# The head of a decoder layer on one core: x in four loads, the c row spread by two K = 1 products, and another order on ScalarE and VectorE

## The chip, the core and the metric

The kernel runs on one core of a Trainium2 chip. The metric is the device time of one execution in microseconds (us). Before the change three executions took 319.98, 317.79 and 318.15 us, a median of 318.15. Engines are called as in the profile: PE is TensorE (matmuls), PEld its weight loads, DVE is VectorE, ACT is ScalarE, POOL is GpSimd, SP is SyncE; a "q" behind a name (SPq, ACTq) is the engine's own instruction queue, where loads are issued.

## What is computed

One layer of a hybrid attention block on 512 tokens of width 1024:

```python
mod = silu(c) @ w_ada + b_ada                  # c: (1, 1024), w_ada: (1024, 3072)
shift, scale, gate = split(mod, 3)
h = rms_norm(x, norm_gain) * (1 + scale) + shift
proj = h @ w_in                                # q, k, v, gates of two head groups
...                                            # sliding-window attention, sparse attention
out = x + gate * (concat(A, B) @ w_out)
```

All data are f32. Products that need the precision are made in three passes of rounded operands: high by high, high by low and low by high, where the low part is what rounding left.

## The kernel before

The program has a head, a middle and a tail. The head (lines 290 to 413) computes h for eight tiles of 128 channels, transposed (channel on the partition, 512 tokens in the row), and at once the first projection (q, k, v of group A, 768 columns, `first_proj`). The middle holds the other projections and the 44 attention slots, put between each other by a planner with costs in us, and ordered by the framework's scheduler. The tail (lines 1002 to 1018) is the last product and the residual.

All the code of the head stands under `in_order(tc)`: on each engine the instructions keep the order in which they are written. What matters of it here:

- **Loads.** SP issues them all: x in eight loads of 256 KB (L297), `first` (L298: the column of c, the biases, the gain and the identity), `bias` (L299), then for k = 0 to 3 the modulation weights of tile k in two loads of 512 KB (L205 for k = 0 and 1, L209 for the rest) and the projection weights `wst` of tile k in one of 384 KB (L213), and between the first two tiles the row of c, spread over 128 partitions by the load itself (`scrow`, L305, 512 KB written). A load whose buffer or semaphore is still in use holds SP, and so all loads behind it.
- **Sums of squares** (L325 to L330): ACT squares each tile of x, DVE adds four tiles at a time into `sacc`, and PE sums `sacc` over the partitions into `pr`. The last tile is done in halves. DVE then works out the reciprocal root in 8 small steps (`rsqrt`, L101 to L108), and PE turns it into a row for all partitions (`rbp`, L352).
- **Modulation.** Tiles 0 and 1 get theirs from PE: `mod_pe` (L230) multiplies by the column silu(c), ACT copies the result out as `macc` (L233), `mod_col` (L250) sums it over the partitions, and `mod_ab` (L255, L256) makes the two columns `AB`. Tiles 2 to 7 get theirs from DVE: `mod_rows` (L222) multiplies the weights, which lie in rows, by `scrow`, the row silu(c), and adds up, two instructions of 1024 elements for each tile. `scrow` is made at L373 (tanh on ACT) and L376 (DVE). The same row is used once more for `gate` in the middle (L690).
- **Tile k** (`new_tile`): ACT makes `hh` (h rounded) and `hf` (h) from the scaled x (`h_high`, L276); DVE does `mod_rows` of the next tile, `hl` = hf - hh (L279), scales the next tile of x (L270), and makes `swl`, the low part of the next weights (L265), whose high part `swh` is ACT's (L262).
- **First projection of tile k**: three passes n = 0, 1, 2 on PE (L286, L287), which need (hh, swh), (hh, swl) and (hl, swh). Behind pass 0 of tile 0 stands `mod_pe(1)`, behind pass 1 of tile 0 `mod_col(1)`.
- **Dummies** (L312): products of zeros on PE, counts in `ND`, written where PE would have nothing to do.
- **The bias line** (L343 to L348): one small product `pl`, two ACT copies and two stores to DRAM; the middle reads the line back from there.

## Time and profile before

| | us |
|---|---|
| median of three executions | 318.15 |
| the profiled execution, its own time | 317.5 |
| its span, first to last instruction | 315.7 |
| start of the first product of the head's projection (L286, tile 0) | 16.28 |
| start of the first `mod_rows` | 21.93 |
| first product of the middle's projections (L469) | 53.81 |

The profiled execution took 317.5 us, of which 315.7 are the span of its instructions; 1.8 lie around it. Times in the trace are us from the span's start. A row of the timeline is: start, duration, engine, line, operation, output <- input, shapes, count, and in brackets how long the engine stood idle before it and who released it. A row that merges several instructions (x2, x3) gives the time from the first's start to the last's end. The mean granted clock of PE over the span is 0.998.

### The profile page before, as it was taken

To read this page: it belongs to the slowest core of one execution; us is meant where nothing else is said; L and a number is where in the kernel's file an instruction comes from. 1 tells how busy PE (TensorE), PEld (TensorE's weight loads), DVE (VectorE), ACT (ScalarE), POOL (GpSimd) and SP (SyncE) were. 2 spreads that over 40 slices of the span, in tenths; PEclk is the share of its full clock that TensorE was granted. 3 is DMA by queue.
4 is the path that set the end of the run, shared out by engine and by line. 5 is a ranking of instruction groups with operands and counts; after the bars stand their busy time and mean duration, and the time that the engine had idled before them with its cause. 6 is when DMAs were issued, how large, how long until landed. Compare 5 with 4: busy or idle time off the path is not lost.

```text
span 315.7 us, 5779 instructions
## 1 busy us (share of the span) xinstructions
PE 306.7 (97%) x2097; PEld 250.9 (79%) x2098; DVE 237.2 (75%) x657; ACT 195.8 (62%) x472; POOL 3.9 (1%) x21
## 2 busy tenths in 40 slices
PE   8989999999999999999999999999999999999995
PEld 3568888788988999889873878788788878788883
DVE  3689999999966658898997998988686686544220
ACT  5576457668967674767917767788685867503000
POOL 0000000000000000000000000000000000000000
PEclk9999999999999999999999999999999999999999
DMA  7999967900390808170653004222420220243201
GB/s 242 375 412 411 408 233 223 322 2 0 100 335 22 282 2 275 32 260 2 197 187 118 1 2 133 69 66 70 134 69 0 69 66 3 81 151 111 90 33 66
DMA packets 28087, 44.63 MB, mean 141 GB/s; under 512 B 1771, under 2 KB 19340, under 8 KB 28060
## 3 DMA queue, kind: packets, MB, share of 16 engines
q1 hardware_dynamic: 26908, 42.18, 38.5%
q10 hardware_dynamic: 1152, 2.10, 2.1%
q8 instruction: 16, 0.26, 0.3%
q14 instruction: 11, 0.09, 0.1%
HBM read 42.13 MB, written 2.14 MB: 140 GB/s over the span
## 4 chain that ended last, share of the span: by engine, by line
PE 76%; DVE 10%; DMA 6%; ACT 4%; issue 2%; SPq 1%; POOL 0%; ACTq 0%; DVEq 0%; POOLq 0%
PE pj L469 29%; PE pj L459 9%; PE po L930 7%; PE s L855 7%; PE sq L286 7%; PE pt L913 4%; PE skv L287 3%; PE pt L903 3%; DMA wst_ring<-in_w_qkv_a 3%; PE s L588 3%; DVE qs L520 2%; DMA xTp<-in_xT 2%; DMA raw<-in_w_gate 2%; DVE kTb L538 1%; DVE wl L174 1%
## 5 line engine op out<-in xcount | busy, mean ns | idle before, releaser
L173 ACT ACTIVATE wh<-raw 128x512 fp32r<-128x512 f32 (+1 forms) x52 | 31.2, 636 | 13.5 <-PE pj L469 13.4
L174 DVE TENSOR_TENSOR wl<-raw,wh 128x512 fp32r<-128x512 f32 (+1 forms) x52 | 34.8, 689 | 5.2 <-ACT wh L173 3.4
L459 PE MATMUL pj<-wh,hh 128*128 128x256 f32 (+1 forms) x128 | 37.0, 289 | 0.0
L459 PE MATMUL pj<-wl,hh 128*128 128x256 f32 (+1 forms) x128 | 36.7, 287 | 0.1
L459 PE MATMUL pj<-wh,hl 128*128 128x256 f32 (+1 forms) x128 | 36.6, 286 | 0.0
L867 ACT ACTIVATE pp<-pp,nm 128x256 f32<-128x256 f32 (+2 forms) x48 | 29.3, 613 | 6.6 <-DVE nm L860 6.4
L469 PE MATMUL pj<-hh,wh 128*128 128x512 f32 x80 | 32.2, 402 | 0.0
L469 PE MATMUL pj<-hh,wl 128*128 128x512 f32 x80 | 32.0, 400 | 0.0
L469 PE MATMUL pj<-hl,wh 128*128 128x512 f32 x80 | 31.8, 398 | 0.0
L860 DVE CUSTOM_DVE_ANT_0 pp<-s,bias 128x256 f32<-128x256 f32 (+2 forms) x48 | 25.5, 551 | 3.6 <-PE s L855 3.5
L469 PE MATMUL pj<-yl,wh 128*128 128x512 f32 x64 | 25.3, 398 | 0.0
L469 PE MATMUL pj<-yh,wh 128*128 128x512 f32 x64 | 25.2, 396 | 0.0
L1017 DVE SCALAR_TENSOR_TENSOR fin<-pj,gate,xr 128x512 f32<-128x512 f32 x8 | 6.0, 751 | 25.5 <-PE pj L469 25.5
L469 PE MATMUL pj<-yh,wl 128*128 128x512 f32 x64 | 25.1, 394 | 0.0
L459 PEld LDWEIGHTS pj<-wl,hh 128*128 128x128 f32 x128 | 24.1, 188 | 0.4 <-DVE wl L174 0.3
L459 PEld LDWEIGHTS pj<-wh,hh 128*128 128x128 f32 x128 | 24.1, 188 | 0.3 <-issue 0.2
L459 PEld LDWEIGHTS pj<-wh,hl 128*128 128x128 f32 x128 | 24.1, 188 | 0.2 <-issue 0.2
L855 PE MATMUL s<-kTb,qs 128*128 128x256 f32 (+2 forms) x96 | 23.5, 356 | 0.0
L888 DVE TENSOR_SCALAR pp<-pp,rr,grev 128x256 f32<-128x256 f32 (+2 forms) x48 | 21.1, 476 | 0.7
L914 ACT COPY ptT<-pt 128x384 f32<-128x384 f32 (+1 forms) x32 | 15.7, 530 | 7.0 <-PE pt L913 6.7
L904 ACT COPY ptT<-pt 128x512 f32<-128x512 f32 (+1 forms) x28 | 15.5, 552 | 5.2 <-PE pt L903 4.9
L469 PEld LDWEIGHTS pj<-hh,wh 128*128 128x128 f32 x80 | 15.0, 188 | 3.8 <-issue 1.2
(232 smaller groups left out, 703.7 us busy)
## 6 DMA issues: line engine op xcount, KB each, us to landing
ada_ring<-in_w_ada_rows SPq DMA_DIRECT2D x12, 512.0 KB, 9.3
raw<-in_w_cmp SPq DMA_DIRECT2D x8, 512.0 KB, 6.5
raw<-in_w_gate SPq DMA_DIRECT2D x8, 512.0 KB, 5.6
raw<-in_w_o SPq DMA_DIRECT2D x8, 512.0 KB, 3.8
wst_ring<-in_w_qkv_a SPq DMA_DIRECT2D x8, 384.0 KB, 9.0
xTp<-in_xT SPq DMA_DIRECT2D x8, 256.0 KB, 4.9
ada_ring<-in_w_ada_cols SPq DMA_DIRECT2D x4, 512.0 KB, 7.3
bias<-line_d SPq DMA_DIRECT2D x8, 256.0 KB, 3.3
```

What stands on the lines that cost most here:

```text
L173: ACT.activation(wh, src, AF.Copy)
L174: DVE.tensor_tensor(wl, src, wh.bitcast(F32), op=OP.subtract)
L286: PE.matmul(pj_q[tb], lt, w[:, 0:512], start=f, stop=l, skip_group_check=True)
L459: PE.matmul(bank[:, t * n:(t + 1) * n], h[:, tb * 128:(tb + 1) * 128], w[:, k % 2, :], start=k == 0 and m == 0, stop=k == 7 and m == 2)
L469: PE.matmul(bank, w, h, start=k == 0 and m == 0, stop=k == 7 and m == 2)
L855: PE.matmul(ps, qs[h][:, 128 * i:128 * i + 128], k[:, hl_, lo:lo + w], start=hl_ == 0, stop=hl_ == 1)
L860: DVE.tensor_tensor_reduce(out=P[:, g, 0:w], in0=ps, in1=bt, scale=1.0, scalar=init, op0=OP.add, op1=OP.min, accum_out=nm[:, g:g + 1])
L867: ACT.activation(P[:, g, 0:e], P[:, g, 0:e], AF.Exp, bias=nm[:, g:g + 1], scale=-1.0, accum_out=dn[:, g:g + 1])
L888: DVE.tensor_scalar(v, v, rr[:, g:g + 1], gates[:, g, br:br + 1], op0=OP.mult, op1=OP.mult)
L904: ACT.copy(T[:, :, 0:nb, :], rev(pt[:, 0:2 * nb * 128].rearrange("p (g b q) -> p g b q", g=2, b=nb)))
L914: ACT.copy(T[:, 0:nb, :], rev(pt[:, 0:nb * 128].rearrange("p (b q) -> p b q", b=nb)))
L930: PE.matmul(o[64 * g:64 * g + 64, 128 * i:128 * i + 128], vb[:, 64 * g:64 * g + 64], sl["T"][g][:, b, :], start=first_of and b == 0, stop= ...
```

## The change

- x is laid out in DRAM as four blocks [128, 2, 512] and loaded in four loads of 512 KB, 4 KB for each partition, in place of eight with 2 KB. (The residual's loads of x in the tail read 2 KB out of each 4 KB.)
- `first` is padded from 168 to 256 columns.
- The row of c is loaded once, to one partition (4 KB), by ACT's own queue ahead of everything on ACT. ACT's tanh and DVE's product that make silu(c) run on this one partition ahead of the squares. PE multiplies a column of ones with K = 1 by the row, two products of 512 columns, into the banks `pj_q[0]` and `pj_q[1]`, and ACT copies them to `scrow` on all partitions behind `th`.
- `bias` is loaded behind the modulation weights of tile 0. Its product `pl` moves behind `mod_col(0)` into `pj_q[3]`, its copies and stores behind `hh(0)` and `hf(0)`.
- `weights_high(1)` (swh of tile 1) is written behind `mod_pe(1)`, so that ACT's copy `macc(1)` comes ahead of it; `weights_low(1)` (swl of tile 1) is written behind `mod_ab(1)`, so on DVE it comes behind `AB` of tile 1 and ahead of the first `mod_rows`.
- The dummies go from (20, 2, 2, 3, 4) to (10, 2, 2, 1, 2, 2); the sixth number is a group behind the K = 1 products.

```diff
-ND = (20, 2, 2, 3, 4)
+ND = (10, 2, 2, 1, 2, 2)
...
-        for k in range(8):
-            SP.dma_start(xT[k], A["xT"][k])
+        ACT.dma_start(scrow[0:1, :], A["c"])
+        for k in range(4):
+            SP.dma_start(xTp[:, 2 * k:2 * k + 2], A["xT"][k])
         SP.dma_start(first, A["first"])
-        SP.dma_start(bl, A["bias"])
         for k in range(NR):
             load_ada(k)
+            if k == 0:
+                SP.dma_start(bl, A["bias"])
             load_wst(k)
-            if k == 0:
-                src = A["c"]
-                SP.dma_start(scrow, bass.AP(tensor=src.tensor, offset=src.offset, ap=[[0, 128], [1, D]]))
...
         dummies(ND[0])
+        throw = T2(F32, "throw"), T2(F32, "throw")
+        for e in range(2):
+            v = scrow[0:1, 512 * e:512 * e + 512]
+            ACT.activation(throw[e][0:1, :], v, AF.Tanh, scale=0.5)
+            DVE.scalar_tensor_tensor(v, throw[e][0:1, :], 1.0, v, op0=OP.add, op1=OP.mult)
+        for e in range(2):
+            PE.matmul(pj_q[e], one_row, scrow[0:1, 512 * e:512 * e + 512], start=True, stop=True)
+        dummies(ND[5])
...
         ACT.activation(th, cT, AF.Tanh, scale=0.5)
+        for e in range(2):
+            ACT.activation(scrow[:, 512 * e:512 * e + 512], pj_q[e], AF.Copy)
...
-        PE.matmul(pl, bl[:, NEAR:NEAR + 40], bl[:, 0:NEAR], start=True, stop=True)
         dummies(ND[1])
-        ACT.copy(lsb[0:40, LINE - NEAR:LINE], pl)
...
         mod_col(0)
+        PE.matmul(pl, bl[:, NEAR:NEAR + 40], bl[:, 0:NEAR], start=True, stop=True)
         dummies(ND[3])
...
         h_low(0)
-        weights_high(1)
-        weights_low(1)
-        throw = T2(F32, "throw"), T2(F32, "throw")
-        for e in range(2):
-            ACT.activation(throw[e], scrow[:, 512 * e:512 * e + 512], AF.Tanh, scale=0.5)
-        for e in range(2):
-            v = scrow[:, 512 * e:512 * e + 512]
-            DVE.scalar_tensor_tensor(v, throw[e], 1.0, v, op0=OP.add, op1=OP.mult)
...
                 if k == 0 and n == 0:
                     mod_pe(1)
+                    weights_high(1)
                 if k < 7 and n == 1:
                     if k == 0:
                         mod_col(1)
                         mod_ab(1)
+                        weights_low(1)
                     new_tile(k + 1)
```

Three places show how the instructions now stand.

DVE, from hl of tile 0 to the first `mod_rows` (ISA rows; in the changed kernel lines are shifted by 2), before and then now:

```order
L279 TENSOR_TENSOR hl_84<-hf,hh_76 128x512
L265 TENSOR_TENSOR swl<-wst_ring,swh 128x768
L376 SCALAR_TENSOR_TENSOR scrow<-throw,scrow 128x512 x2
L255 TENSOR_TENSOR AB<-pj,first 128x1
L256 SCALAR_TENSOR_TENSOR AB<-pj,prm_98,first 128x1
L222 ISA ada_ring,AB<-ada_ring,scrow,first 128x1024
```

The same place on DVE in the changed kernel:

```order
L281 TENSOR_TENSOR hl_86<-hf,hh_78 128x512
L257 TENSOR_TENSOR AB<-pj,first 128x1
L258 SCALAR_TENSOR_TENSOR AB<-pj,prm_100,first 128x1
L267 TENSOR_TENSOR swl<-wst_ring,swh 128x768
L224 ISA ada_ring,AB<-ada_ring,scrow,first 128x1024
```

The two products of the row have left this place, and swl of tile 1 has moved from ahead of AB to behind it.

ACT, from h of tile 0 to h of tile 1, before and then now:

```order
L363 ACTIVATE hh_76<-xTp,AB 128x256 x2
L364 ACTIVATE rb<-pj 128x512
L365 ACTIVATE hf<-xTp,AB 128x512
L262 ACTIVATE swh<-wst_ring 128x768
L373 ACTIVATE throw<-scrow 128x512 x2
L233 ACTIVATE macc_309<-pj 128x256
L276 ACTIVATE hh_77<-xTp,AB 128x256 x2
```

The same place on ACT in the changed kernel:

```order
L370 ACTIVATE hh_78<-xTp,AB 128x256 x2
L371 COPY raw<-sq_124 40x256
L372 ACTIVATE rb<-pj 128x512
L373 ACTIVATE hf<-xTp,AB 128x512
L377 COPY raw<-raw 8x384
L235 ACTIVATE macc_295<-pj 128x256
L264 ACTIVATE swh<-wst_ring 128x768
L278 ACTIVATE hh_79<-xTp,AB 128x256 x2
```

The tanh of the row has left, macc of tile 1 is ahead of swh of tile 1, and the two copies of the bias line have come in between.

PE, from the first dummies to the sums of squares, now (before, twenty dummies stood there and nothing else):

```order
L313 MATMUL skv_125<-zero 128x512
L322 MATMUL sq_121<-scrow,one_row 128x512
L322 MATMUL sq_122<-scrow,one_row 128x512
L313 LDWEIGHTS zero
L313 MATMUL skv_125<-zero 128x512
L313 LDWEIGHTS zero
L313 MATMUL skv_125<-zero 128x512
L339 MATMUL pj<-ones,sq 128x1 x4
```

The two K = 1 products (operands `one_row` and one partition of `scrow`) stand on PE ahead of both sums of squares. In the middle, the scheduler orders the instructions of about 60 to 125 us a little differently: attention products and projection products change places with each other, with none added or left out; from about 130 us on the order is the same on all engines.

## The prediction

> **What bounds the kernel now.** I read the page first, then the stages, then the chain of waits, and only then single instructions. Two rows of stages: the head's inner tiles, and a piece of the middle (columns: stretch, its length, busy time of PE, PEld, DVE, ACT, POOL with counts, granted PE clock, DMA share, GB/s).

> ```profile
> 22.00:48.00 26.00, 25.96 (x144) 21.63 (x143) 26.00 (x42) 15.23 (x24) 0.00 (x0) 1.00 0.90 346
> 62.00:80.00 18.00, 17.01 (x126) 15.44 (x124) 17.39 (x40) 13.36 (x33) 0.68 (x4) 1.00 0.02 8
> ```

> From 22 to 48 us DVE is busy 26.00 of 26.00 us. PE's 25.96 look the same, but a busy PE counts the pipelined ends of its products; which of the two waits is read from single rows. Here are DVE from hl of tile 0 to the first `mod_rows`, the last `mod_rows` with its hl, and a place on PE:

> ```profile
> 17.94 0.69 DVE L279 TENSOR_TENSOR hl<-hf,hh 128x512 fp32r<-128x512 f32 x1
> 19.66 0.96 DVE L265 TENSOR_TENSOR swl<-wst_ring,swh 128x768 fp32r<-128x768 f32 x1 [1.03 <-ACT swh L262]
> 20.54 1.28 DVE L376 SCALAR_TENSOR_TENSOR scrow<-throw,scrow 128x512 f32<-128x512 f32 x2
> ...
> 21.93 1.28 DVE L222 CUSTOM_DVE_ANT_0 ada_ring<-ada_ring,scrow,first 128x1024 f32<-128x1024 f32 x1
> ...
> 44.66 1.27 DVE L222 CUSTOM_DVE_ANT_0 ada_ring<-ada_ring,scrow,first 128x1024 f32<-128x1024 f32 x1
> ...
> 47.13 0.68 DVE L279 TENSOR_TENSOR hl<-hf,hh 128x512 fp32r<-128x512 f32 x1
> ```
> ```profile
> 47.60 0.28 PE L287 MATMUL skv<-swl,hh 128*128 128x256 f32 x1
> 47.87 0.50 PE L286 MATMUL sq<-swh,hl 128*128 128x512 f32 x1
> ```

> Five tiles take DVE 44.66 - 21.93 = 22.73 us, 4.55 each, with no gap. PE starts a pair (L286, L287) every 0.35 us, 12 pairs in 4.2 us for a tile; at 47.60 it has its last pair of pass 1 and starts pass 2 at 47.87, when hl (47.13 + 0.68) is there. So in the tiles DVE leads, and the head ends when DVE's chain does: **what counts is the start of the first `mod_rows`, 21.93**. What held that back is in the chain of waits (start, length, what):

> ```profile
> 4.01 5.36 DMA xTp<-in_xT
> 9.39 0.33 SPq L205
> 9.76 8.99 DMA wst_ring<-in_w_qkv_a
> ...
> 19.53 1.13 ACT throw L373 x2
> 20.67 0.28 ACT macc L233
> 20.99 0.61 PE pj L250 x4
> ```

> The last x landed at 4.01 + 5.36 = 9.37. The weights of tile 1 landed at 18.75; swh, the tanh of the row and then macc(1) followed in ACT's order, so PE's `mod_col(1)` began at 20.99.

> **The change part by part.** *The end of x.* Rows of the stages of loading, and of what ACT, DVE and PE do with x:

> ```profile
> 1.50:3.50 2.00, 2.00 (x6) 0.76 (x5) 0.00 (x0) 0.65 (x2) 0.00 (x0) 1.00 0.86 262
> 3.50:5.00 1.50, 1.50 (x5) 0.45 (x3) 0.35 (x1) 1.12 (x2) 0.00 (x0) 1.00 0.76 247
> 10.50:19.00 8.50, 7.83 (x65) 4.73 (x67) 5.89 (x23) 4.60 (x9) 0.00 (x0) 1.00 1.03 416
> ```
> ```profile
> 8.70 1.49 DVE L327 TENSOR_TENSOR sacc<-sacc,sq 128x512 f32<-128x512 f32 x2 [1.01 <-ACT sq L325]
> 10.29 0.76 DVE L327 TENSOR_TENSOR sacc<-sacc,sq 128x256 f32<-128x256 f32 x2
> ```
> ```profile
> 7.43 0.63 ACT L325 ACTIVATE sacc<-xTp 128x512 f32<-128x512 f32 x1 [0.61 <-DMA xTp<-in_xT]
> ```
> ```profile
> 10.77 1.05 PE L330 MATMUL pj<-ones,sacc 128*128 128x1 f32 x8 [0.58 <-DVE sacc L327]
> ...
> 16.28 0.51 PE L286 MATMUL sq<-swh,hh 128*128 128x512 f32 x1 [0.34 <-ACT hh L363]
> ```

> x is 2.10 MB. Loads with 2 KB rows ran at 262 and 247 GB/s up to 5.0, loads with 4 and 3 KB rows later at 416. All of it at 416 from 1.8 on, plus 0.3 to land, would end at 7.2; no better than now at 9.4. I take the first two rates up to 5.0 (0.52 + 0.37 = 0.89 MB), then 416 for the other 1.21 MB (2.9 us), and 0.2 to land: 8.1, nearer the fast end because the slow stretch is the start-up. But the last load now brings two tiles: after it come a square (0.63), its sum (half of 1.49, 0.74) and the first half's sum (0.38), 1.75 us to the start of PE's sum, where 10.77 - 9.37 = 1.40 stood. So PE's sum starts at 9.9, 0.9 earlier (9.0 to 11.15 for the two bounds). The steps from there to the first product at 16.28 are a chain of small ones and stay as they are.

> *The row of c.* The tanh's 1.13 us leave ACT's place ahead of macc(1), and its products' 1.28 leave DVE's ahead of `AB`. They come back ahead of the squares, on one partition, DVE's part ahead of its first sum; I cost them the same, since the length of a row and not the partitions set it in this pair of rows (8 partitions, 384 columns, against 40 and 256):

> ```profile
> 12.41 0.36 ACT L345 COPY raw<-sq 40x256 f32<-40x256 f32 x1 [2.19 <-PE sq L343]
> 12.81 0.51 ACT L346 COPY raw<-raw 8x384 f32<-8x384 f32 x1
> 13.98 0.38 ACT L233 ACTIVATE macc<-pj 128x256 f32<-128x256 f32 x1 [0.66 <-PE pj L230]
> ```

> The cover is the wait for x: if c lands at 2.9, the tanh ends at 4.0, where the first pair of x lands now anyway, and six squares end at 7.8, just ahead of x's last pair. So x at 7.2 would be used from 7.8 only, which caps this gain at 1.2; c later than 3.2 costs its lateness one for one. No row shows so small a load; those of 256 KB that ACT issues near the end take 2.9 us (line of the DMA issues: KB each, median us to landing):

> ```profile
> xr<-in_xT ACTq DMA_DIRECT2D x8, 256.0 KB, 2.9
> ```

> Issued at 0.8 that is 3.7 at the worst side (0.5 lost); at the best 1.8, before which no byte of x moves either (nothing more won). I take 2.9. [...]

> The copies of the row from PSUM, two of 512 columns at no more than a square's 0.63, lie in ACT's 2.19 + 0.66 us of idleness ahead of macc(0), so nothing; without that cover they would cost 1.3 us.

> *The loads behind x.* All come 1.3 us earlier by x, and those behind the old 512 KB of `scrow` another 1.3 (at 416 GB/s); the padding of `first` gives 0.1 back. The weights of tile 1 then land near 16.3, and ACT does not wait for them. SP's stores of the bias line wait for an ACT copy that ends at about 17.9, ahead of the 19.4 at which SP came there before, so the later loads on SP's queue aren't held.

> *Up to the first `mod_rows`.* ACT's last step of tile 0 and PE's `mod_pe(1)` ahead of pass 1 stand in these rows:

> ```profile
> 17.10 0.80 ACT L365 ACTIVATE hf<-xTp,AB 128x512 f32<-128x512 f32 x1
> ```
> ```profile
> 17.87 1.07 PE L230 MATMUL pj<-ada_ring,scz 128*32 128x256 f32 x16
> ```

> Pass 0 of tile 0 starts at 16.28 - 0.9 = 15.4. The bias copies put rb, hf and hl(0) 0.36 later (the copy with 40 partitions) and what follows hf 0.51 more: hl(0), 17.94 + 0.69 before, is done at 18.1, and ACT is free for macc(1) at 17.9 - 0.9 + 0.36 + 0.51 = 17.9. `mod_pe(1)` ends at 18.94 - 0.9 = 18.05, so macc(1) is there at 18.45, ahead of pass 1's end. So `mod_col(1)` starts as soon as pass 1, four pairs or 1.4 us, is through: 18.94 + 1.4 = 20.35 in the old order, now 19.5. From the start of `mod_col` to behind AB it was 21.93 - 20.99 = 0.94, so AB is done at 20.45. There the edit takes part of its gain back: **swl of tile 1, 0.88 from start to next start, now stands between AB and `mod_rows`**, while DVE idles from 18.1 to 20.2. The first `mod_rows` starts at 21.35 in place of 21.93: **0.6 earlier**, 0.3 less than PE's sum. PE's third pass gains more (19.95 against 21.46), but meets DVE's chain again in tile 1.

> *Dummies and K = 1 products.* Twelve dummies less; a product costs PE only where something waits behind it, which is a rival below.

> *The middle* gets the same work in another order. I take 0. PE's idle time there is 0.99 us in the row of 62 to 80 at the top, and that of these two:

> ```profile
> 125.00:150.00 25.00, 24.06 (x209) 22.70 (x208) 22.70 (x59) 18.03 (x41) 0.19 (x1) 1.00 0.32 112
> 150.00:175.00 25.00, 24.38 (x145) 16.81 (x144) 21.28 (x62) 15.82 (x41) 0.00 (x0) 1.00 0.46 159
> ```

> 2.55 us together (25 less 24.06 and 24.38); an order gains no more of what these rows show, and I let a bad one lose 1.3, half of that.

> **Sum.** 0.6 less (bounds -0.7, if x ends as now, to 0.9, for c's cap). The profiled execution took 317.5, so 316.9; the median of the runs, 318.15, gives 317.5. I say **317.5**.

> **The rivals.** *(a) The sums of PE come late: slower.* The K = 1 products stand ahead of both sums on PE, and PE's clock starts slow:

> ```profile
> 6.75 0.15 PEld L312 LDWEIGHTS <-zero 128*128 128x128 bf16 x1 [0.28 <-issue]
> 7.07 0.96 PEld L312 LDWEIGHTS <-zero 128*128 128x128 bf16 x5 [0.17 <-issue]
> 11.75 0.62 PE L343 MATMUL sq<-raw 33*40 33x256 f32 x2
> ```

> Dummies come every 0.43 us (0.15 and 0.28 of idleness of the weight load) up to 7.07, and five in 0.96 us from there. The f32 product of 256 columns takes two parts, 0.21 apart, so one of 512 takes 0.86 fast, 1.7 slow. Ten dummies end at 5.5. If the clock rises at 7.07 as before, the products end near 8, in time for 9.9. If it stays slow, they end at 8.9, two dummies at 9.8, the first sum (0.95 before) at 11.7, two dummies at 12.5: 2.6 late, all of it on the path. The rise decides this: from about 8 us on PE is the later one. With the 0.6 of the forecast lost and more: 318.15 - 0.6 + 2.6 = 320.2. Against it: PE is no emptier up to 5.5 than before. [...]

> *(b) x lands no earlier.* The same bytes on the same 16 engines; for it speaks the slow stretch up to 5.0, against it that 0.76 and 0.86 of DMA share there are idleness and not load. The first `mod_rows` then comes 0.7 later than before: 318.9.

> *(c) The new order of the middle closes most of its gaps*: 2 of 2.55 us: 315.5. For it: 62 to 80 has DVE nearly full and PE idle for 1 us. Against: an order that a scheduler makes has no reason to.

> **How the numbers follow.** Chances: the forecast 0.62, (a) 0.12, (b) 0.13, (c) 0.13. The forecast with the bounds of the head (-0.7 to 0.9) and half of the middle's is 316.0 to 319.0; to leave out no more than 2 in 10, the range goes half-way into (a) and (c): **315.6 to 319.6**. A measurement of this kernel can tell about 1%, 3.2 us, from no change. Faster by more needs (c) and the best head: 0.07. Slower by more needs (a) with a bad order: 0.05. Within 1%: 0.88.

> **What would show it.** Right: ACT's last square ends near 9.5; L286 of tile 0 starts near 15.4; PE doesn't wait ahead of `mod_col(1)`; DVE idles about 2 us ahead of AB of tile 1 and then has swl; the first `mod_rows` starts near 21.35; tiles 4.55 us apart; the first L469 near 53.2. Wrong: a first `mod_rows` ahead of 20.9 or behind 22.5, tiles closer than 4.5 us, or a middle from 53 to 271 us that changes by over 1.3.

## The result, and the profile after

| | executions | median us | lowest to highest | ratio to before, 95% interval |
|---|---|---|---|---|
| before | 15 | 318.05 | 317.02 to 319.98 | |
| after | 15 | 321.66 | 319.04 to 323.98 | 1.0081 [1.0053, 1.0108] |

The change costs 0.8%, about 2.6 us by the ratio and 3.6 between the medians, where 0.6 less was forecast. The profiled execution of after took 322.68 us, with a span of 320.9 (before 317.5 and 315.7). Ratios leave out executions more than 1.5% above the fastest of their kernel; that goes for one execution of after and of e1 and for two each of e2, e8 and e9, and the profile of e9 is of such a one (325.1 us).

The page's row of the granted clock, 40 slices of 8 us, in tenths of full speed:

```profile
PEclk9569999999999999999999999999999999999998
```

Slices two and three (8 to 24 us) show 5 and 6: half speed for most of them. The granted clock rises at 4.99 us, falls at 8.40 and rises again at 22.05. The first step is 3.41 us and the second four times that; a step of 3.41 us is called a window here. The stages around it (the columns are those of the prediction's stages; the number ahead of the last two is the granted clock):

```profile
5.00:8.40 3.40, 3.40 (x14) 1.43 (x12) 2.08 (x3) 1.69 (x4) 0.00 (x0) 1.00 0.92 323
8.40:22.00 13.60, 12.17 (x52) 7.58 (x52) 7.26 (x25) 7.30 (x16) 0.00 (x0) 0.50 1.02 391
...
24.00:28.00 4.00, 4.00 (x25) 3.52 (x24) 2.60 (x6) 2.96 (x6) 0.00 (x0) 1.00 0.37 119
28.00:50.00 22.00, 21.82 (x117) 17.62 (x116) 22.00 (x34) 12.25 (x20) 0.00 (x0) 1.00 0.99 355
```

The profiled execution is one of four with a share (the mean granted clock over the span) of 0.976, 322.2 to 322.7 us. Two have 0.982 (321.5 and 321.7 us), five 0.986 to 0.989 (319.0 to 320.2 us), and four have 0.998 or 1.00 and still took 321.5 to 324.0 us.

For 13.6 us the granted clock is 0.50, in the very stretch in which every step of the head waits for a short product of PE. From 28 us on DVE is full again (22.00 of 22.00), as before. PE itself (start, length, what, number of products; L313 are the dummies, called fillers from here on):

```profile
1.35 4.11 PE L313 MATMUL skv<-zero 128*128 128x512 bf16 x10 [1.35 <-DVE wst_ring L296]
5.39 1.98 PE L322 MATMUL sq<-scrow,one_row 1*128 1x512 f32 x4
7.30 0.61 PE L313 MATMUL skv<-zero 128*128 128x512 bf16 x2
7.75 1.30 PE L339 MATMUL pj<-ones,sq 128*128 128x1 f32 x8
8.91 1.01 PE L313 MATMUL skv<-zero 128*128 128x512 bf16 x2
11.35 1.86 PE L339 MATMUL pj<-ones,sacc 128*128 128x1 f32 x8 [1.43 <-DVE sacc L336]
```

PE was busy without a break through the window that ended at 8.40, but what it did in the middle of it were the two products with one row (L322, "1x512"). Behind it the same sum that took 1.05 us before (L330, x8) takes 1.86. The chain of waits up to `mod_pe(1)`:

```profile
1.65 6.43 DMA xTp<-in_xT
...
11.35 1.86 PE pj L339 x8
13.22 0.88 PE skv L313 x2
14.09 1.87 PE pj L232 x16
15.96 1.05 PE pj L358 x4
17.01 0.85 PE skv L313 x2
17.86 0.65 PE pj L252 x4
18.50 1.00 PE sq L361 x2
...
22.41 1.00 PE pj L232 x16
```

Before, this piece of the chain held x, the weights of tile 1, ACT's rounding, tanh and macc. Now it is PE alone, one slow product behind the other, the fillers too. The x on it is the third load, landed at 8.08; the fourth landed at 9.34, when DVE was still adding up the third (9.28 on), so the two come to nearly the same. DVE behind that:

```profile
21.52 0.69 DVE L281 TENSOR_TENSOR hl<-hf,hh 128x512 fp32r<-128x512 f32 x1
25.40 0.16 DVE L257 TENSOR_TENSOR AB<-pj,first 128x1 f32<-128x1 f32 x1 [3.18 <-PE pj L252]
25.47 0.21 DVE L258 SCALAR_TENSOR_TENSOR AB<-pj,prm,first 128x1 f32<-128x1 f32 x1
25.60 0.95 DVE L267 TENSOR_TENSOR swl<-wst_ring,swh 128x768 fp32r<-128x768 f32 x1
26.46 1.28 DVE L224 CUSTOM_DVE_ANT_0 ada_ring<-ada_ring,scrow,first 128x1024 f32<-128x1024 f32 x1
...
49.20 1.27 DVE L224 CUSTOM_DVE_ANT_0 ada_ring<-ada_ring,scrow,first 128x1024 f32<-128x1024 f32 x1
```

DVE idles 3.18 us ahead of A and B of tile 1, then does swl, then `mod_rows`, in the order that was foretold, but at 26.46 and not at 21.35. The span cut at starts of instructions, all from the traces (`e3` and `e5` are experiments, told below; before, the first product of the middle starts at 53.65 by its own row, and 53.81 is where the chain has it):

| stretch, us | before | after | e3 | e5 |
|---|---|---|---|---|
| start to PE's second sum of squares | 10.77 | 11.35 | 11.15 | 11.29 |
| to pass 0 of tile 0 | 5.51 | 8.25 | 5.40 | 5.50 |
| to `mod_col(1)` | 4.71 | 5.26 | 4.12 | 4.83 |
| to the first `mod_rows` | 0.94 | 1.60 | 1.60 | 0.94 |
| to the first product of the middle | 31.72 | 31.80 | 31.77 | 31.72 |
| to the end | 262.06 | 262.63 | 262.86 | 261.77 |
| span | 315.71 | 320.89 | 316.90 | 316.05 |

Of the 5.2 us between the two profiled spans 4.5 lie ahead of the first `mod_rows`, and 2.7 of these in the one stretch from PE's second sum to pass 0.

### The profile page after: what moved, and what is told of

Same layout as the page of the kernel before. It is cut to its first block, busy times and chain, and to the rows that moved or that the text cites. A ratio compares the mean times of both kernels' runs of the same rounds, so it can differ in the third digit from the quotient of the medians.

```text
span 320.9 us, 5766 instructions
## 1 busy us (share of the span) xinstructions
PE 310.8 (97%) x2090; PEld 253.1 (79%) x2090; DVE 237.4 (74%) x658; ACT 196.5 (61%) x474; POOL 3.9 (1%) x21
## 4 chain that ended last, share of the span: by engine, by line
PE 63%; DVE 22%; DMA 6%; issue 4%; ACT 3%; SPq 0%; DVEq 0%; ACTq 0%
PE pj L474 24%; PE po L935 7%; PE pj L464 7%; PE s L860 7%; PE pt L918 4%; DVE wl L176 4%; PE pt L908 3%; PE s L593 2%; DMA wst_ring<-in_w_qkv_a 2%; DVE ada_ring L224 2%; DVE qs L525 2%; DMA xTp<-in_xT 2%; DMA raw<-in_w_gate 2%; PE po L941 1%; DVE pa L865 1%
## 5 line engine op out<-in xcount | busy, mean ns | idle before, releaser
L1022 DVE SCALAR_TENSOR_TENSOR fin<-pj,gate,xr 128x512 f32<-128x512 f32 x8 | 6.0, 751 | 25.4 <-PE pj L474 25.4
L909 ACT COPY ptT<-pt 128x512 f32<-128x512 f32 (+1 forms) x28 | 15.4, 552 | 7.1 <-PE pt L908 6.0
## 6 DMA issues: line engine op xcount, KB each, us to landing
bias<-line_d SPq DMA_DIRECT2D x8, 256.0 KB, 4.1
```

The costliest lines, as they stand in the source:

```text
L909: ACT.copy(T[:, :, 0:nb, :], rev(pt[:, 0:2 * nb * 128].rearrange("p (g b q) -> p g b q", g=2, b=nb)))
```

## The experiments

Each kernel was timed beside the kernel before on the same chip; its ratio is to that. Three theories were named ahead of the first kernels. **A**: the products with one row don't keep the clock up; behind a window of 3.41 us with them in it, it falls, though PE is busy. **B**: only the share of PE's busy time decides, and the rows don't matter. **C**: the clock is not the cause; loads or order are.

**e1_fill**: the changed kernel with ten fillers, not two, between the sums of squares.

```
-ND = (10, 2, 2, 1, 2, 2)
+ND = (10, 2, 2, 1, 10, 2)
```

> The changed kernel with 8 more dummies (10 in place of 2) behind the first sum of squares; the K = 1 products stay. Theory A (products with K = 1 do not keep PE's clock up: the 3.4 us in which they stand count as idle, and the clock falls there, whatever stands behind): the clock still falls near 8.4 us in most executions, 320 to 322 us. Theory B (what counts is how much of the time PE works on anything; the idle 1.9 us ahead of the second sum and the missing dummies let it fall): the clock holds, the first mod_rows starts at 22.3 to 23, 318.2 to 319.3 us. Theory C (the clock is not the cause, but the loads and the order are): as the changed kernel, 321 to 322 us, even where the clock holds.

Measured: 321.69 us (320.09 to 326.0), ratio 1.0072 [1.003, 1.0114]: no better. PE's stages (columns: PE busy, granted clock, DMA share, GB/s) and its first rows:

```profile
5.00:8.40 3.40, 3.40 (x5) 1.00 0.91 333
8.40:16.80 8.40, 8.40 (x27) 1.00 1.03 378
```
```profile
1.35 4.45 PE L313 MATMUL skv<-zero 128*128 128x512 bf16 x10 [1.35 <-DVE wst_ring L296]
5.73 3.77 PE L322 MATMUL sq<-scrow,one_row 1*128 1x512 f32 x4
```

Here the clock column must not be believed: the trace records changes of the clock, the first in this execution is its rise at 16.86 us, and what lies ahead of the first is shown as 1.00. The durations tell the truth: four parts of the row products take 3.77 us (1.98 in after, at full speed), so the clock was low from the start. PE was busy for 8.40 of 8.40 us from 8.40 on and stayed slow. Theory B falls.

**e2_k128**: the changed kernel, with 128 rows in the two row products: the same row of c, which DVE's product now writes to `crow`, and 127 rows of zeros.

```
-one_row = con.tile([1, 128], F32, name="one_row")
+one_row = con.tile([128, 128], F32, name="one_row")
+crow = con.tile([128, D], F32, name="crow")          # zeroed ahead
-    PE.matmul(pj_q[e], one_row, scrow[0:1, ...], ...)
+    PE.matmul(pj_q[e], one_row, crow[:, ...], ...)
```

> The changed kernel with the two products of the row made with K = 128: the row in partition 0 of a tile whose other 127 rows are zeros, the same columns and the same place. Theory A: the 3.4 us with the products now count as work; the clock falls one such window later at the earliest, or where PE idles ahead of the second sum: 319 to 320.5 us, with 0 to 3 slow windows where the changed kernel has 2 to 4. Theory B: K does not matter, as the changed kernel, 321 to 322 us. Theory C: 321 to 322 us.

**e3_k128_fill**: both edits, 128 rows and ten fillers.

> Both edits together: products with K = 128 and 10 dummies behind the first sum. Theory A and theory B: the clock holds from its rise on, the first mod_rows starts at 22.3 to 23 us, 318.2 to 319.3 us in all. Theory C: 321 to 322 us with the clock up.

Measured: e2 319.78 us (317.38 to 322.81), ratio 1.0015 [0.9976, 1.0054]; e3 318.80 (318.2 to 319.65), ratio 0.9994 [0.9971, 1.0017], with a granted clock of 0.998 or more in all ten executions. PE's stages, e2 first:

```profile
6.00:12.90 6.90, 5.10 (x34) 1.00 1.02 356
12.90:16.30 3.40, 3.18 (x23) 0.50 1.03 408
```
```profile
6.00:12.90 6.90, 6.67 (x42) 1.00 1.02 355
12.90:16.30 3.40, 2.91 (x28) 1.00 1.03 413
```

With 128 rows but little filler, PE is busy for 5.10 of 6.90 us and loses the clock for one window at 12.90; with both, 6.67 of 6.90, it keeps it. e3 does the whole of the change's work in the change's order, and its first `mod_rows` starts at 22.27 and not at 26.46:

```profile
22.27 1.28 DVE L225 CUSTOM_DVE_ANT_0 ada_ring<-ada_ring,scrow,first 128x1024 f32<-128x1024 f32 x1
```

So C falls, and what is left is A; e9 and e12 below test it alone. In the profiled executions **the clock is 4.2 of the head's 4.5 us.** As the ratios go, 1.0081 against 0.9994, it is 0.9% of the time.

**e4_x4**: the kernel before, with x in four loads and nothing else.

> The kernel before with one part of the change: x in four loads of 4 KB rows (and the residual's loads of it in the tail with 2 KB rows at a pitch of 4 KB). If four loads bring x no earlier (as the changed kernel's trace has it: 9.3 us): the second sum starts 0.4 to 0.6 us later, since two tiles now hang on the last load, 318.2 to 318.7 us. If the larger rows are faster by themselves, and the changed kernel lost that to something else (the load of c on ACT's queue, or an earlier start of the modulation weights): x lands by 8.5 us, and the kernel is 0 to 0.5 us faster than before.

Measured: 318.53 us (317.16 to 320.6), ratio 0.9986 [0.9955, 1.0016]: nothing that can be told from none. ACT's squares:

```profile
7.95 0.61 ACT L325 ACTIVATE sq<-xTp 128x512 f32<-128x512 f32 x1
8.86 1.24 ACT L325 ACTIVATE sq<-xTp 128x512 f32<-128x512 f32 x3 [0.30 <-DMA xTp<-in_xT]
```

The last pair of x is there at 8.86 and PE's second sum starts at 10.80, against 10.77 before: what the last load won, two tiles in it took back. Whether it won anything isn't shown: with eight loads the last x lands between 8.85 (e12) and 9.87 us (e5).

**e5_before_fill**: the kernel before, with six more fillers between the sums.

```
-ND = (20, 2, 2, 3, 4)
+ND = (20, 2, 2, 3, 10)
```

> The kernel before with six more filler products between the two sums of squares (ND[4] 4 to 10) and nothing else. Theory A (the granted clock of the head is what separates executions, and the changed kernel lost it through the products with one row): the filler closes PE's idle stretch between the sums, so the clock stays up in all executions; the mix of clock shares that the kernel before shows (0.998, 0.994, 0.989) becomes 0.998 throughout, the first mod_rows stays within 0.3 us of 21.93, and the median falls from 318.4 to about 317.2, ratio 0.996. Rival (the slower executions of the kernel before come from something else than idle PE ahead of 12 us): the mix of clock shares and the median stay, ratio 1.00. Six more instructions in the head also move the written-out order of the middle; if that order is worth something by itself, the time between the first middle product and the end differs from 262.06 us by up to 1.3 us either way.

Measured: **317.20 us** (316.66 to 318.68, 12 executions), ratio 0.9958 [0.9937, 0.998]. The 35 executions of the kernel before that were timed beside it show clock shares of 0.989 (10), 0.994 or 0.995 (21) and 0.998 or more (4); a window of 3.41 us at half speed takes 0.54% off the share, so by this estimate these are two, one and none. All 12 of e5 show 0.997 or more. Theory A foretold this: the kernel before lost, by the same estimate, a window or two in most of its executions as well, and with six more products of zeros none of the 12 did. The first `mod_rows` lay at 22.56, since x was later by 0.5 in this execution, and the stretches behind are those of before.

**e6_swl**: e3 with `weights_low(1)` back ahead of A and B of tile 1.

```
                     mod_pe(1)
                     weights_high(1)
+                    weights_low(1)
...
                         mod_ab(1)
-                        weights_low(1)
```

> The changed kernel with 128 rows in the spread and the filler (the one that held its clock), and the low half of the second tile's weights put back ahead of that tile's A and B. Theory: what is left of its head behind the kernel before (22.27 against 21.93 at the first mod_rows) is the 0.95 us of that subtraction between A and B and mod_rows; ahead of A and B it runs from the end of the rounding at 20.56, in time in which VectorE waits, so the first mod_rows comes at 21.65, 0.6 us earlier, and the first middle product with it (53.4 against 54.04); the rest to the end stays or moves by up to 1 us with the middle's order: span 315.5 to 317. Rival: the gain is lost because A and B then wait for the subtraction as long as mod_rows did before (first mod_rows within 0.2 of 22.27), span 316.9.

Measured: 318.73 us (318.27 to 319.22), ratio 1.0017 [0.9995, 1.0038]. From PE's second sum to the first `mod_rows` it is 10.49 us in place of 11.12 in e3: the 0.6 are there, as expected. They are not in the time: from the first product of the middle to the end it is 263.20 in place of 262.86, though only this one instruction was moved.

**e7_order**: e5 with tile 1's rounding behind `mod_pe(1)`, so that macc need not wait for it.

```
-        weights_high(1)
-        weights_low(1)
...
                     mod_pe(1)
+                    weights_high(1)
+                    weights_low(1)
```

> The kernel before with the filler and one part of the change alone: the second tile's weights are rounded behind its modulation sums, so that macc no longer waits for the rounding; c, x and the bias stay as before. Theory: macc runs at about 19.2 in place of 20.57, the second tile's mod_col comes when pass 1 ends (about 20.4), VectorE's subtraction (about 21.3) is then what A and B wait for, first mod_rows at 21.5 (21.93 before), so the order alone is worth 0.4 us of the head. Rival: silu(c)'s spread row, which still takes its two Tanh on ScalarE and two products on VectorE in the same stretch, leaves the first mod_rows where it was, 21.9; then the order and the spread's removal are only worth something together.

Measured: 317.22 us (316.9 to 317.97), ratio 0.9965 [0.9945, 0.9984]. The first `mod_rows` starts at 21.17, 10.34 us behind PE's second sum (e5: 11.27). The median is that of e5: what the head wins here (0.93) is not in the time, and from the first product of the middle to the end e7 takes 262.29 where e5 takes 261.77.

**e10_bias** is e7 with the change's place for the bias row, its two copies behind `hh` and hl of tile 0; **e11_spread** is e7 with c's row spread as in e2 (128 rows), with ten fillers at the start and two behind the products in place of twenty.

> The kernel before with the filler and the weights' order, and the change's place for the bias row added: its load behind the first modulation weights, its product behind the first mod_col, its two copies and two stores behind. Theory M1 (the 0.8 us that all kernels with the whole change take longer from the first middle product to the end, 262.5 to 263.2 against 261.8 to 262.3, come from the bias row's later copies and stores): 262.8 here, time 317.8 to 318.2. Theory M2 (they come from the written-out order of the middle, which any edit of the head shifts): somewhere between 261.7 and 263.2, not bound to this edit; time 317.2 with the head at 52.9.

> The kernel before with the filler and the weights' order, and the spread added: c as one row by the other queue, two products with 128 rows, the spread load, the two wide Tanh and two wide products gone. Theory: ScalarE and VectorE lose 1.13 and 1.28 us of work ahead of the second tile's A and B, so macc and the rounding can run by 0.3 us earlier, but the second tile's mod_col stays behind pass 1 on PE (20.3), and the first mod_rows comes at 21.2 as without the spread: worth nothing, 317.2. Rival: the 512 KB less in the queue ahead of the second tile's weights and the free VectorE bring it to 20.8 or less, 316.8. If the middle's 0.8 us come with the spread (M3), 262.8 from the first middle product to the end and 318.0.

Measured: e10 318.03 us (317.56 to 318.56), ratio 0.9998 [0.9987, 1.001]; e11 317.71 (317.15 to 318.55), ratio 0.9983 [0.9966, 1.0001]. ACT of e7, then of e10:

```profile
17.05 0.80 ACT L365 ACTIVATE hf<-xTp,AB 128x512 f32<-128x512 f32 x1
17.76 1.14 ACT L371 ACTIVATE throw<-scrow 128x512 f32<-128x512 f32 x2
18.95 0.39 ACT L233 ACTIVATE macc<-pj 128x256 f32<-128x256 f32 x1
19.23 0.84 ACT L262 ACTIVATE swh<-wst_ring 128x768 fp32r<-128x768 f32 x1
```
```profile
16.65 0.35 ACT L361 COPY raw<-sq 40x256 f32<-40x256 f32 x1
...
18.23 0.51 ACT L367 COPY raw<-raw 8x384 f32<-8x384 f32 x1
18.76 1.15 ACT L372 ACTIVATE throw<-scrow 128x512 f32<-128x512 f32 x2
19.82 0.37 ACT L233 ACTIVATE macc<-pj 128x256 f32<-128x256 f32 x1
20.09 0.83 ACT L262 ACTIVATE swh<-wst_ring 128x768 fp32r<-128x768 f32 x1
```

The two copies of the bias row used to lie in ACT's idle stretch behind the squares. In the new place they stand ahead of the tanh, macc and the rounding swh. macc is not what counts: `mod_col(1)` starts 9.36 us behind PE's second sum, and 9.49 in e7. swh starts 9.01 behind it in place of 8.40, and swl, A and B and `mod_rows` follow it on DVE: the first `mod_rows` moves from 10.34 to 10.94. That is 0.6 lost, of the 1.05 us between the two ratios, whose intervals don't meet; the rest isn't placed. The spread wins nothing here: 10.37 in e11. M1's time (317.8 to 318.2) came true, but by luck: its cause falls, for the middle does not take longer (262.31 us from the first middle product to the end in e10, 262.29 in e7, 262.45 in e11).

**e8_k32_fill**: e3 with 32 rows in the row products, the same order on every engine.

> As the kernel with 128 rows in the spread and the filler, with the same order of instructions on every engine but 32 rows in the two row products (one with data, 31 of zeros). Theory A1 (what the throttle counts grows with the rows that a product uses, so a quarter of the rows is too little): the clock falls in the window that holds them as it did with one row, half clock for one to four windows of 3.41 us ahead of 20 us, time 319.5 to 322. Theory A2 (one row alone is special; a row group of 32 already counts as busy): the clock holds as with 128 rows, clock share 0.998 in all runs and 318.8 median.

Measured: 318.87 us (318.45 to 325.33), ratio 1.003 [1.0006, 1.0054]. Neither quite: of the eight executions in its ratio six are as e3's (318.45 to 318.91), and two lost one window (320.08 and 320.59, share 0.995). The other two of its ten took 325.2 and 325.3, which no kernel with 128 rows came to. In e3 and e6, with 128 rows, none of twenty lost one.

**e9_k1_alone** and **e12_k128_alone**: the kernel before with the fillers of e5, and with two row products of zeros, whose result is thrown away, in place of the last ten fillers of the start. They differ in the rows of that product alone, and PE's order is the same.

```
 dummies(ND[0])                       # 10 in place of 20
+for e in range(2):
+    PE.matmul(pj_q[2 + e], one_row, zrow, start=True, stop=True)   # 1 row in e9, 128 in e12
```

> The kernel before with ten more fillers taken as follows: of the twenty at the start the last ten give way to two row products of one row each (zeros, result thrown away, waiting for nothing), and the filler between the two sums has its six more. No other part of the change is in it. Theory A: two products with one row in place of ten fillers take the granted clock away again, half clock in at least one window of 3.41 us between 7 and 20 us in most executions, median 318.3 to 321.5. Rival (the clock was lost by the wait for c, by PE's later sums or by the order, none of which is in here): clock share 0.998 or more throughout and 317.2, as with the fillers.

> The same kernel with 128 rows of zeros in the two products, the same order of instructions on every engine. Theory A: the clock holds in all executions, 317.2 median (317.0 to 317.6). Rival: no difference from the one with one row.

Measured: e9 318.81 us (318.38 to 325.13), ratio 1.0025 [1.0003, 1.0046]; e12 **317.13** (316.7 to 318.95), ratio 0.9963 [0.9933, 0.9992]. PE in e9, then in e12:

```profile
1.90 4.45 PE L316 MATMUL skv<-zero 128*128 128x512 bf16 x10 [1.90 <-DVE wst_ring L298]
6.27 3.78 PE L320 MATMUL sq<-zrow,one_row 1*128 1x512 f32 x4
9.98 1.87 PE L336 MATMUL pj<-ones,sq 128*128 128x1 f32 x8
```
```profile
1.91 4.45 PE L316 MATMUL skv<-zero 128*128 128x512 bf16 x10 [1.91 <-DVE wst_ring L298]
6.15 2.42 PE L320 MATMUL sq<-zrow,one_row 128*128 128x512 f32 x4
8.41 0.95 PE L336 MATMUL pj<-ones,sq 128*128 128x1 f32 x8
```

Both start slow (4.45 us for ten fillers; the next ten of e12, behind the rise, take 2.32). In e12 the clock rises at 7.24, within the row products, and the sum behind them takes 0.95 us; in this execution of e9 it rises at 24.32 and the sum takes 1.87. Of the eight executions in e9's ratio seven show a share of 0.994 or 0.995, one window lost, and none of e12's is below 0.997. A rise that comes late is not in the share (1.00 in this execution of e9), so four of e12's, with 1.00 and 317.8 to 318.95 us, may have started slow for longer. Even so one row against 128, with all else equal, is worth 0.6% of the time, and theory A needs no wait for c, no later sum and no new order.

## Why the prediction was wrong

**The step that failed** is the one on *dummies and K = 1 products*: "a product costs PE only where something waits behind it". It counted a filler as work that may be left out. But what the fillers held up here was the clock: twelve fillers less, and products of one row in their stead, let it fall for 13.65 us, four windows, in the profiled execution. That made the stretch from PE's sum to pass 0 longer by 2.74 us. Both halves count: the fillers put back alone don't help (e1, 1.0072), 128 rows alone still lose a window (e2, in its profile), and both together bring 0.9994 (e3).

**Rival (a)** had this price (2.6 us, 320.2 in all) but not the mechanism. It was to be decided by a rise of the clock later than 8 us; in the profiled execution the clock rose at 4.99, earlier than before (6.95), and the row products ran fast: 1.98 us for both. It then *fell* at 8.40. The steps in after's trace are whole windows: 4.99 to 8.40 is 3.41, 8.40 to 22.05 four times that. PE's row of 5.00 to 8.40 is busy for 3.40 of 3.40 us, and the clock fell at its end. The prediction asked for the rise alone, and its "PE is no emptier up to 5.5 than before" looked at busy time, which does not tell rows. Other executions may have gone the way of (a): the four of after with shares of 0.998 and 1.00 look like e1's profile (323.9 us, share 0.998), whose clock rose at 16.86 only. They have no trace, so that stays open.

**x** was to land at 8.1 and PE's sum to start at 9.9. The last landing in after's trace is 9.34 (before 9.38), and the sum starts at 11.35: rival (b), whose condition came true. Here the term was wrong by its rate. I took 416 GB/s behind 5.0 us from a later stretch with rows of 3 and 4 KB. The stretch in question in after, and then in before (clock, DMA share and GB/s stand at the end):

```profile
5.00:9.40 4.40, 4.40 (x18) 2.04 (x16) 2.19 (x4) 2.58 (x6) 0.00 (x0) 0.89 0.93 323
```
```profile
5.00:9.40 4.40, 4.40 (x22) 2.35 (x21) 2.42 (x4) 3.14 (x6) 0.00 (x0) 1.00 1.03 343
```

It ran at 323 and 343 GB/s, and part of that belongs to the loads behind x, which SP now issues sooner (from 2.85 us, 4.49 before). The row of before was in its trace ahead of the result. The cap by two tiles in the last load was right: 2.01 us from landing to PE's sum in place of 1.40 (1.75 foretold).

**c** came earlier than the 2.9 that I took: issued at 0.74, it was there by 2.58, 1.84 us later at most. ACT's first rows:

```profile
1.28 1.28 ACT L319 ACT_TABLE_LOAD   x1 [1.28 <-PEq L1086]
2.58 1.15 ACT L319 ACTIVATE throw<-scrow 1x512 f32<-1x512 f32 x2
...
8.10 0.63 ACT L334 ACTIVATE sacc<-xTp 128x512 f32<-128x512 f32 x1 [1.41 <-DMA xTp<-in_xT]
...
10.61 1.06 ACT L345 ACTIVATE scrow<-sq 128x512 f32<-128x512 f32 x2
```

The tanh starts as its table is loaded, at 2.58, and takes the foretold time (1.15 against 1.13). The copies of the row (L345) lie in ACT's idle time, as foretold.

**The order up to the first `mod_rows`** was right, and e3, with its clock up, shows the sizes: from pass 0 to `mod_col(1)` 4.12 us (19.5 - 15.4 = 4.1 foretold), and 1.60 from there, where 20.45 - 19.5 + 0.88 = 1.83 were foretold: swl eats the gain. From PE's sum to `mod_rows` it comes to 11.12, against 11.16 before, so the order as a whole is worth nothing. That macc no longer waits for the rounding helps only where tile 1's weights land late: in e12, in the old order, the rounding began at 18.30 without waiting for them, and `mod_rows` came 10.22 us behind PE's sum, no later than e7's 10.34. *The bias copies* were booked at 0.36 and 0.51 and hidden; behind the spread they are, but alone (e10) they cost 0.6.

**SP's queue**: it was not to be held. It was: SP waits 9.7 us for PE ahead of the load `rest` (L307), until 25.4, and the DMA share falls to 0.37 from 24 to 28 us. Yet the five tiles lie (49.20 - 26.46) / 5 = 4.55 us apart, so nothing waited for it.

**The middle** was put at 0, within +1.3 and -2.55. The middle with the tail behind it is 0.57 longer in the profiled execution (262.63 against 262.06), and 262.5 to 263.2 in all kernels that hold the whole change, against 261.8 to 262.3 in e4, e5, e7, e9 and e12. With the clock held the change as a whole stands at ratio 0.9994 (e3), where the kernel before with its clock held stands at 0.9958 (e5): 0.36%, about 1.1 us. Their intervals overlap, but those of e6 (e3 with one instruction moved, 1.0017) and e5 don't. The profiled executions put 1.09 us of it into the middle (262.86 - 261.77). Rival (c), the middle's gaps closed, did not occur. That its order does it is likely, since e6 moved one instruction in the head and the middle changed by 0.34; which rule of the scheduler, and which edit, was not settled.

**What is better than both kernels**: the kernel before with six more fillers (e5, 0.9958 [0.9937, 0.998]); e7 and e12 are the same within their intervals. Nothing of the change is needed for it.

## What to carry to other kernels

Ask of a filler what it holds up before counting it as free to remove; on PE here that was the clock, and products with one row did not hold it, though the profile showed PE busy (3.40 of 3.40 us in after, up to the fall at 8.40). Read the clock at the start of a program from the durations of known products (ten fillers: 4.45 us in e1, where the column shows 1.00, and 2.32 behind the rise in e12), and over several executions, for the first rise lay at 4.99 us in after, 6.95 in before, 7.24 in e12, 16.86 in e1 and 24.32 in e9. For a transfer, take the rate of the very stretch (323 and 343 GB/s here), and not of a faster stretch near by (416).
